# Layer 1's change of sweeps: whose queue stores the finished rows, and which rows are read first

## The chip, the cores and the metric

The kernel runs on one core of a Trainium2 chip. A core has a matrix engine (PE, with its weight loads shown apart as PEld), a vector engine (DVE), an activation engine (ACT), a general engine (POOL) and a sync engine (SP). Each works through its own list of instructions in order and waits on semaphores for the others. Transfers between HBM and the on-chip memory are issued from an engine's queue, here SP's or POOL's, and carried by 16 DMA engines that all queues share. The metric is the device time of one execution in microseconds; lower is better.

## The reference

The program is a two-layer encoder trunk over 2048 rows of 1024 values. Layer 0 is windowed attention beside a gated spatial mixer. Layer 1, which the change touches, is a gated linear recurrence that runs over the sequence in both directions:

```python
def odd_mixer(h, w_in, conv_w, conv_b, w_a, b_a, w_x, b_x, lam, w_out):
    xr, g = jnp.split(h @ w_in, 2, axis=-1)
    xr = centred_depthwise_conv(xr, conv_w, conv_b)
    y = (rg_lru(xr, w_a[0], b_a[0], w_x[0], b_x[0], lam[0], reverse=False)
         + rg_lru(xr, w_a[1], b_a[1], w_x[1], b_x[1], lam[1], reverse=True))
    y = y.astype(h.dtype) * jax.nn.silu(g)
    return y @ w_out
# each layer: x = layer_norm(DEEPNORM_ALPHA * x + gate * mixer(x * (1 + scale) + shift), ln_g, ln_b)
```

`rg_lru` is the scan h[s] = a[s] h[s-1] + b[s]. All of it is in float32; the kernel makes each float32 product from three matmuls of split operands (`mm3`).

## The kernel before

The sequence is cut into four tiles of 512 rows (t = 0 to 3), the width into eight chunks of 128 channels (k or g = 0 to 7). Layer 1 has two sweeps.

**The first sweep** goes forward, t = 0 to 3. For each tile it projects, convolves and computes the gates; it scans forward with the carry from the tile before, and scans backward within the tile, since the carry from behind isn't known yet. For tiles 0 to 2 it stores what the second sweep needs: for even chunks the raw scan inputs (`a_d`, `b_d`), the forward result (`f_d`) and the gate (`g_d`); for odd chunks the finished sum and its carry factor (`u_d`, `v_d`). At the last tile the backward carry is known to be zero, so its rows are finished on the spot by `back(NT - 1, ...)`: DVE multiplies the sum by the gate (line 1034), two columns of it are stored to `y_d` (line 1040, 128 partitions of two values: because of the convolution a tile of scans lies two rows early, so these two belong to tile 2), and ACT and DVE split the other 512 (lines 154 and 155) into the pair `ahi`, `alo` that PE multiplies by the output weights.

**The second sweep** goes backward, t = 2, 1, 0. `load_y(t)` reads a tile back chunk by chunk. An even chunk reads `at`, `bt`, `ft`, `gt` (line 1106), finishes the backward scan on DVE (line 1113), adds on POOL (lines 1116 and 1117), gates on DVE (line 1118); an odd chunk reads `ut`, `vt` and applies the carry on DVE (line 1127). At t = 2 both also read two columns from `y_d` (line 1130). Then ACT and DVE split the result (lines 154, 155). Each name has two buffers, so two chunks of a kind can be ahead. PE then multiplies, for each of four blocks of 128 rows (b) and two halves of the output (n), all eight chunks into one PSUM bank; DVE adds the residual rows `z` (`residual_tile` reads them from `x1_d`, 512 KB each, line 1144; the sums are lines 1164, 1177, 1193) and normalises (`norm_rows`, lines 614 to 625, its last line stores to the output).

**The change of sweeps** lies between them. The program there reads, in this order: the last output weights `wo` are loaded (line 1079), `back(NT - 1, 1, ...)` finishes the second four chunks of tile 3, the memory of the first sweep is given up (`se.close()`) and the pool `op` of the second takes its place, the four residual rows `z` of tile 3 are read, `load_y(2)` follows, and PE's matmuls of tile 3 on chunks 4 to 7.

Loads and stores all go through SP's queue here, in the order of SP's list: an instruction that waits holds what stands behind it. A tile of `op` waits for the last use of whatever lay at its address, and where it lies depends on the order in which names first appear in the pool. The engines' lists are not written by hand: the framework orders each list by its own estimate of when instructions can run, so that a small edit moves instructions on all engines.

Of the kernel before, what the change touches and what calls it, by code (L numbers as in the profile page):

```python
# [20 lines left out]
NT = S // C  # L21
# [32 lines left out]
def kernel(  # L54
# [27 lines left out]
    nc = tc.nc  # L82
# [5 lines left out]
    store = nc.sync.dma_start  # L88
# [24 lines left out]
    y_d = dram.tile([128, KD, 2], F32, name="y_d")  # L113
# [39 lines left out]
    def split(hi, lo, src):  # L153
        act(out=hi, in_=src, func=AF.Copy)  # L154
        tt(out=lo, in0=src, in1=hi.bitcast(F32), op=ALU.subtract)  # L155
# [83 lines left out]
    for i in range(2):  # L239
        nc.gpsimd.dma_start(out=vrow0[24 + 8 * i:32 + 8 * i].rearrange("k (a q) -> k a q", a=4),  # L240
                            in_=ada_b[1, i * D:i * D + D].rearrange("(a k q) -> k a q", a=4, q=32))
# [276 lines left out]
    def act_pair():  # L518
        hi = cp.tile([128, 2, C], F32R, tag="act", bufs=12, name="ahi")
        lo = cp.tile([128, 2, C], F32R, tag="act", bufs=12, name="alo")  # L520
        return hi, lo
# [322 lines left out]
    for t in range(NT):  # L844
        y = sgate(t, hT)
# [41 lines left out]
    def span(t):  # L887
        j0 = 2 if t == 0 else 0
        return j0, (514 if t == NT - 1 else 512) - j0
# [134 lines left out]
    def back(t, s, res, G):  # L1024
        j0, W = span(t)
        w = slice(j0, j0 + W)
        tok = slice(t * C - 2 + j0, t * C - 2 + j0 + W)
        for i in range(4):
            g = 4 * s + i
            if t < NT - 1 and g % 2 == 0:  # L1030
                store(out=g_d[:, g, tok], in_=G[i][:, w])
                continue
            y, A = res[i]
            stt(out=y[:, w], in0=y[:, w], scalar=0.5, in1=G[i][:, w], op0=ALU.mult, op1=ALU.mult)
            if t < NT - 1:
                store(out=u_d[:, g // 2, tok], in_=y[:, w])
                stt(out=A[:, w], in0=A[:, w], scalar=0.5, in1=G[i][:, w], op0=ALU.mult, op1=ALU.mult)
                store(out=v_d[:, g // 2, tok], in_=A[:, w])
                continue
            store(out=y_d[:, g, :], in_=y[:, 0:2])  # L1040
            if i % 2 == 0:
                yp = act_pair()
            split(yp[0][:, i % 2], yp[1][:, i % 2], y[:, 2:514])
            y3[0].append(yp[0][:, i % 2])
            y3[1].append(yp[1][:, i % 2])

    for t in range(NT):
        if t < NT - 1:
            for s in range(2):
                X = x_job(t, hT, s)  # L1050
                if s == 1:
                    nxt = build1(t + 1)
                f = front(t, s, X)
                back(t, s, f, g_job(t, hT, s))
            hT = nxt
        else:
            X0 = x_job(t, hT, 0)
            f0 = front(t, 0, X0)
            X1 = x_job(t, hT, 1)
            f1 = front(t, 1, X1)  # L1060
            sf.close()
            back(t, 0, f0, g_job(t, hT, 0))
            G1 = g_job(t, hT, 1)
# [25 lines left out]
    for k in range(4, KD):  # L1089
        for n in range(2):  # L1090
            resident(oq, n, k)
    back(NT - 1, 1, f1, G1)
    cr = oq.tile([128, NT, KD // 2], F32, name="cr")
    nc.vector.tensor_copy(cr[:, NT - 2], carry_b[:, NT - 1, 1::2])
# [1 line left out]
        tt(out=cr[:, t], in0=first_a[:, t + 1], in1=cr[:, t + 1], op=ALU.mult)  # L1096
        tt(out=cr[:, t], in0=cr[:, t], in1=first_h[:, t + 1], op=ALU.add)

    def load_y(t):
        y = ([], [])  # L1100
        n = C if t < NT - 2 else C - 2
        c0 = t * C

        def fetch(tag, src, k):
            p = op.tile([128, C], F32, tag=tag, bufs=2, name=tag)
            load(out=p[:, 0:n], in_=src[:, k, c0:c0 + n])  # L1106
            return p

        for k in range(KD):
            if k % 2 == 0:  # L1110
                at, bt, ft, gt = (fetch(tag, src, k) for tag, src in (("at", a_d), ("bt", b_d), ("ft", f_d), ("gt", g_d)))
                h = bt[:, 0:n]
                nc.vector.tensor_tensor_scan(out=h[:, ::-1], data0=at[:, 0:n][:, ::-1], data1=h[:, ::-1],  # L1113
                                             initial=carry_b[:, t + 1, k:k + 1], op0=ALU.mult, op1=ALU.add)
                if t > 0:
                    nc.gpsimd.tensor_copy(carry_b[:, t, k:k + 1], bt[:, 0:1])
                nc.gpsimd.tensor_tensor(out=ft[:, 0:n], in0=ft[:, 0:n], in1=h, op=ALU.add)
                stt(out=ft[:, 0:n], in0=ft[:, 0:n], scalar=0.5, in1=gt[:, 0:n], op0=ALU.mult, op1=ALU.mult)
                if t == NT - 2 or k < 4:
                    hi, lo = act_pair()  # L1120
                else:
                    hi, lo = (op.tile([128, 2, C], F32R, tag="act2", bufs=8, name=nm) for nm in ("ahi", "alo"))
            else:
                ft, vt = (fetch(tag, src, k // 2) for tag, src in (("ut", u_d), ("vt", v_d)))
                for u, q0, q1 in ((t, 0, C - 2), (t + 1, C - 2, C)):
                    if u < NT - 1:
                        stt(out=ft[:, q0:q1], in0=vt[:, q0:q1], scalar=cr[:, u, k // 2:k // 2 + 1],  # L1127
                            in1=ft[:, q0:q1], op0=ALU.mult, op1=ALU.add)
            if n < C:
                load(out=ft[:, n:C], in_=y_d[:, k, :])  # L1130
            split(hi[:, k % 2], lo[:, k % 2], ft)
            y[0].append(hi[:, k % 2])
            y[1].append(lo[:, k % 2])
        return y
# [6 lines left out]
    def residual_tile(t, b):  # L1141
        r = t * C + b * 128
        z = op.tile([128, D], F32, tag="z", bufs=6, name="z")
        load(out=z, in_=x1_d[r:r + 128, :])
        return z

    zt = [residual_tile(NT - 1, b) for b in range(4)]
    g_bc = op.tile([128, D], F32, name="g_bc1")
    b_bc = op.tile([128, D], F32, name="b_bc1")
    y2 = load_y(NT - 2)  # L1150
    for k in range(4, KD):
        for n in range(2):
            part_out(ps3[n], wo[n][k], k)
# [14 lines left out]
    zt = [residual_tile(NT - 2, b) for b in range(4)]  # L1168
# [11 lines left out]
    for t in range(NT - 3, -1, -1):  # L1180
        y = load_y(t)
        for b0, n in ((0, 0), (0, 1), (2, 0), (2, 1)):
            for b in (b0, b0 + 1):
                if n == 0:
                    zt[b] = residual_tile(t, b)
                z = zt[b]
                sl = slice(b * 128, b * 128 + 128)
                ps = bank(pj, "pj") if cnt % 8 < 5 else bank(pm, "pm")
                cnt += 1
                cs = slice(n * C, n * C + C)  # L1190
                for k in range(KD):
                    mm3(ps, y[0][k][:, sl], y[1][k][:, sl], wo[n][k][:, 0], wo[n][k][:, 1], k == 0, k == KD - 1)
                stt(out=z[:, cs], in0=z[:, cs], scalar=ALPHA, in1=ps, op0=ALU.mult, op1=ALU.add)
                if n == 1:
                    finish(t, b, z)
# [29 lines left out]
```

## Time and profile before

| | |
|---|---|
| time, median of 3 executions (range) | 1558.17 us (1556.07 to 1564.16) |
| the profiled execution: its time, its span | 1562.55 us, 1560.8 us |
| PE, PEld busy (share of the span) | 95%, 76% |
| DVE, ACT, POOL busy | 76%, 50%, 26% |
| mean granted clock of TensorE | 0.984 |
| DMA, mean rate over the span | 238 GB/s |

The span runs from the first to the last instruction of the profiled execution; the 1.75 us beside it lie outside. An engine's busy share is an average over stages with different limits. What counts is whether PE, which does nearly all the work that can't be moved, stands still, where, and for whom.

### The profile page before, as it was taken

How to read it: one execution, taken by the hardware profiler on the slowest of the kernel's cores; microseconds unless marked ns; L12 is line 12 of the kernel's file. 1: busy time of each engine (PE TensorE's matmuls, PEld its weight loads, DVE VectorE, ACT ScalarE, POOL GpSimd, SP SyncE). 2: the span in 40 equal slices, each digit the busy share in tenths (PEclk: the TensorE clock that was granted, in tenths of full speed). 3: DMA queues.
4: the chain of work that ended last, by engine and by line, in shares of the span. 5: the costliest groups of instructions: out<-in, count | busy, mean ns of one | idle time of the engine just before them, and what ended most of it. 6: DMA issues, size and time to landing. Idle time of an engine off the chain costs nothing. (4 is left out here: it accounts for less than half of the span.)

```text
span 1560.8 us, 22092 instructions
## 1 busy us (share of the span) xinstructions
PE 1481.5 (95%) x7096; PEld 1185.4 (76%) x7096; DVE 1188.0 (76%) x2180; ACT 783.5 (50%) x1470; POOL 405.1 (26%) x488
## 2 busy tenths in 40 slices
PE   7999999989999999999999999999999999987997
PEld 3887777657777777788887777787777788876886
DVE  4599889745769558976776774987987877789996
ACT  4677767542523332343243327499498486851100
POOL 1023233211005000300120232534645523114321
PEclk9999999999999999999999999999999999998999
DMA  9357776849798989988795699788778667439862
GB/s 346 133 170 219 223 198 187 266 131 298 231 293 302 256 252 300 314 268 266 262 298 177 191 246 294 220 267 282 220 239 288 219 214 237 139 146 340 284 202 88
DMA packets 209211, 370.91 MB, mean 238 GB/s; under 512 B 56616, under 2 KB 103620, under 8 KB 209096
## 3 DMA queue, kind: packets, MB, share of 16 engines
q1 hardware_dynamic: 202344, 354.53, 71.1%
q0 software_dynamic: 6752, 14.98, 3.7%
q8 instruction: 56, 0.92, 0.3%
q14 instruction: 59, 0.48, 0.1%
HBM read 261.96 MB, written 85.97 MB: 223 GB/s over the span
## 5 line engine op out<-in xcount | busy, mean ns | idle before, releaser
L154 ACT ACTIVATE hl<-raw 128x512 fp32r<-128x512 f32 x192 | 118.7, 627 | 224.7 <-DMA raw<-in_ev_w_in_dram 139.0
L158 PE MATMUL pj<-ahi,hl 128*128 128x512 f32 x512 | 200.7, 394 | 1.1 <-DVE gz L753 1.1
L159 PE MATMUL pj<-alo,hl 128*128 128x512 f32 x512 | 201.3, 393 | 0.0
L160 PE MATMUL pj<-ahi,hl 128*128 128x512 f32 x512 | 200.8, 394 | 0.0
L155 DVE TENSOR_TENSOR hl<-raw,hl 128x512 fp32r<-128x512 f32 x192 | 131.9, 696 | 74.3 <-ACT hl L154 74.1
L150 POOL TENSOR_SCALAR rstd<-mv 128x1 f32<-128x1 f32 x32 | 27.4, 857 | 401.6 <-DVE mv L616 289.9
L158 PEld LDWEIGHTS pj<-ahi,hl 128*128 128x128 f32 x512 | 97.4, 190 | 22.2 <-DVE gz L753 1.5
L159 PEld LDWEIGHTS pj<-alo,hl 128*128 128x128 f32 x512 | 97.0, 189 | 20.6
L160 PEld LDWEIGHTS pj<-ahi,hl 128*128 128x128 f32 x512 | 97.0, 189 | 20.6
L465 POOL DMA_DIRECT2D P<-T x112 | 62.4, 566 | 178.9 <-DVE nm L430 77.2
L158 PE MATMUL pj<-wqh,hhi 128*128 128x256 f32 (+1 forms) x256 | 88.3, 349 | 2.5 <-ACT hhi L154 1.7
L430 DVE CUSTOM_DVE_ANT_0 P<-psc,mask,nsink 128x384 f32<-128x384 f32 (+1 forms) x128 | 73.9, 595 | 21.7 <-PE psc L429 21.4
L154 ACT ACTIVATE phl<-praw 128x512 fp32r<-128x512 f32 x56 | 35.4, 632 | 108.2 <-DMA praw<-in_od_w_in_dram 56.6
L159 PE MATMUL pj<-wql,hhi 128*128 128x256 f32 (+1 forms) x256 | 87.9, 344 | 0.0
L160 PE MATMUL pj<-wqh,hlo 128*128 128x512 f32 (+1 forms) x256 | 85.3, 345 | 1.4 <-DVE hlo L155 1.4
L977 DVE SCALAR_TENSOR_TENSOR ii<-ii,xc 128x1024 f32<-128x1024 f32 (+2 forms) x32 | 40.6, 1270 | 58.7 <-ACT ii L971 58.7
L433 ACT ACTIVATE P<-P,nm 128x384 f32<-128x384 f32 (+1 forms) x128 | 76.4, 601 | 11.6 <-DVE nm L430 11.4
L777 POOL TENSOR_TENSOR alo<-hm,ahi 128x512 fp32r<-128x512 f32 x32 | 49.7, 1559 | 119.2 <-DVE hm L776 102.7
L947 DVE SCALAR_TENSOR_TENSOR xc<-X,vcol,xc 128x512 f32<-128x512 f32 (+2 forms) x96 | 77.3, 840 | 0.3
L158 PE MATMUL pm<-xhi,hg 128*128 128x512 f32 (+3 forms) x160 | 56.1, 365 | 13.4 <-ACT xhi L154 6.4
L155 DVE TENSOR_TENSOR phl<-praw,phl 128x512 fp32r<-128x512 f32 x56 | 39.1, 699 | 35.4 <-ACT phl L154 32.1
L775 ACT ACTIVATE ahi<-hm,shift,scale 128x512 fp32r<-128x512 f32 x32 | 25.2, 812 | 75.0 <-DVE hm L774 67.1
(304 smaller groups left out, 4319.2 us busy)
## 6 DMA issues: line engine op xcount, KB each, us to landing
hl<-w_d SPq DMA_DIRECT2D x128, 512.0 KB, 4.8
raw<-in_ev_w_in_dram SPq DMA_DIRECT2D x128, 256.0 KB, 3.9
w_d<-phl SPq DMA_DIRECT2D x40, 512.0 KB, 4.7
aw<-in_ada_w_dram SPq DMA_DIRECT2D x32, 512.0 KB, 6.8
hg<-w_d SPq DMA_DIRECT2D x32, 512.0 KB, 4.0
P<-T SPq DMA_DIRECT2D x104, 96.0 KB, 4.7
P<-T POOLq DMA_DIRECT2D x104, 96.0 KB, 4.2
aw<-in_ada_w_dram SPq DMA_DIRECT2D x8, 1024.0 KB, 7.8
```

Source lines behind the costliest of these rows:

```text
L150: nc.gpsimd.tensor_scalar(out=dst, in0=src, scalar1=mul, scalar2=EPS, op0=ALU.mult, op1=ALU.add)
L154: act(out=hi, in_=src, func=AF.Copy)
L155: tt(out=lo, in0=src, in1=hi.bitcast(F32), op=ALU.subtract)
L158: nc.tensor.matmul(ps, lhsT=ahi, rhs=bhi, start=first, stop=False)
L159: nc.tensor.matmul(ps, lhsT=ahi, rhs=blo, start=False, stop=False)
L160: nc.tensor.matmul(ps, lhsT=alo, rhs=bhi, start=False, stop=last)
L430: nc.vector.tensor_tensor_reduce(out=p[:, g, 0:W], in0=ps[:, 0:W], in1=mask[:, m0:m0 + W], scale=-0.125, scalar=nsink[:, h:h + 1], op0=ALU ...
L433: act(out=p[:, g, 0:W], in_=p[:, g, 0:W], func=AF.Exp, scale=-1.0, bias=nm[:, h:h + 1], accum_out=rs[:, h:h + 1])
L465: dma.dma_start(out=pv[32 * r:32 * r + 32, 0:nb, i], in_=T[32 * i:32 * i + 32, 0:nk].rearrange("p (j r) m -> p r j m", r=4)[:, r])
L777: nc.gpsimd.tensor_tensor(out=lo[:, j], in0=h, in1=hi[:, j].bitcast(F32), op=ALU.subtract)
L947: stt(out=xc[:, w], in0=xt[:, j0 + j:j0 + j + W], scalar=vcol1[:, 8 * j + g:8 * j + g + 1], in1=xc[:, w], op0=ALU.mult, op1=ALU.add)
L977: stt(out=ii[i][:, :, w], in0=ii[i][:, :, w], scalar=1.0, in1=xc[:, None, w].to_broadcast([128, 2, W]), op0=ALU.add, op1=ALU.mult)
```

## The change

Line 1040's store is issued from POOL's queue. `load_y` gets a function that it calls after its first pair of chunks; for t = 2 this is what reads the four residual rows of tile 3, which stood ahead of it. `g_bc1` and `b_bc1` get their place after that call.

```diff
-            store(out=y_d[:, g, :], in_=y[:, 0:2])
+            nc.gpsimd.dma_start(out=y_d[:, g, :], in_=y[:, 0:2])
...
-    def load_y(t):
+    def load_y(t, between=None):
...
         for k in range(KD):
+            if k == 2 and between is not None:
+                between()
             if k % 2 == 0:
...
-    zt = [residual_tile(NT - 1, b) for b in range(4)]
+    zt = []
+    y2 = load_y(NT - 2, lambda: zt.extend(residual_tile(NT - 1, b) for b in range(4)))
     g_bc = op.tile([128, D], F32, name="g_bc1")
     b_bc = op.tile([128, D], F32, name="b_bc1")
-    y2 = load_y(NT - 2)
```

The lines behind are numbered two higher (1113 is 1115, 1118 is 1120, 1127 is 1129, 1144 is 1146, 1164 is 1166).

SP's list, from the last weight load to the first loads of the second sweep. Before:

```order
L1079 DMA wo_7_13377<-wo_d_95 128x1024
L1040 DMA y_d<-T 128x2 x2
L1144 DMA z<-x_d 128x1024 x4
L1106 DMA at<-a_d 128x510
L1106 DMA bt<-b_d 128x510
L1106 DMA ft<-f_d 128x510
L1106 DMA gt<-g_d 128x510
```

The same place on SP with the change:

```order
L1079 DMA wo_7_13377<-wo_d_95 128x1024
L1106 DMA at<-a_d 128x510
L1106 DMA bt<-b_d 128x510
L1106 DMA ft<-f_d 128x510
L1106 DMA gt<-g_d 128x510
L1132 DMA ft<-y_d 128x2
L1106 DMA ut<-u_d 128x510
L1106 DMA vt<-v_d 128x510
L1132 DMA ut<-y_d 128x2
L1146 DMA z<-x_d 128x1024 x4
```

The two stores are gone from SP, and the loads of chunks 0 and 1 stand ahead of the four `z`. The stores of all eight chunks are on POOL now; the end of this stage there reads, with the change:

```order
L1017 TENSOR_TENSOR T<-T 128x514 x2
L1040 DMA y_d<-T 128x2 x2
L1017 TENSOR_TENSOR T<-T 128x514 x2
L1040 DMA y_d<-T 128x2 x2
L1118 COPY carry_b<-bt 128x1
L1119 TENSOR_TENSOR ft<-ft,bt 128x510
```

Each pair of stores stands behind the sums (line 1017) that lead to it, and the first of POOL's work for the second sweep stands behind the last pair.

DVE's list, from the last split of tile 3. Before:

```order
L155 TENSOR_TENSOR alo<-T,ahi 128x512
L1164 SCALAR_TENSOR_TENSOR z<-z,pj 128x512 x2
L614 BN_STATS st_13625<-z 128x6
L1164 SCALAR_TENSOR_TENSOR z<-z,pj 128x512
L614 BN_STATS st_13636<-z 128x6
L1113 SCALAR_TENSOR_TENSOR bt<-at,carry_b,bt 128x510
L1164 SCALAR_TENSOR_TENSOR z<-z,pj 128x512 x2
L1164 SCALAR_TENSOR_TENSOR z<-z,pm 128x512 x2
L1127 SCALAR_TENSOR_TENSOR ut<-vt,cr,ut 128x510
```

With the change:

```order
L155 TENSOR_TENSOR alo<-T,ahi 128x512
L1115 SCALAR_TENSOR_TENSOR bt<-at,carry_b,bt 128x510
L1120 SCALAR_TENSOR_TENSOR ft<-ft,gt 128x510
L1129 SCALAR_TENSOR_TENSOR ut<-vt,cr,ut 128x510
L155 TENSOR_TENSOR alo<-ft,ahi 128x512
L155 TENSOR_TENSOR alo<-ut,ahi 128x512
L1166 SCALAR_TENSOR_TENSOR z<-z,pj 128x512
L614 BN_STATS st_13625<-z 128x6
L1166 SCALAR_TENSOR_TENSOR z<-z,pj 128x512 x2
L614 BN_STATS st_13636<-z 128x6
```

Chunks 0 and 1 of tile 2 are finished ahead of all the residual sums of tile 3; they stood between and behind them. From here to the end PE's list differs too: before, 38 matmuls of tile 2 stood ahead of the first that needs chunk 2, and with the change 48, all of chunks 0 and 1 on all eight banks.

## The prediction

> **What bounds the kernel now.** I began with the stretches of engine time around the change of sweeps. Their columns are the stretch, its length, busy time and instructions of PE, PEld, DVE, ACT and POOL, the granted clock, and the DMA share and rate.
>
> ```profile
> 1400.90:1409.90 9.00, 8.95 (x40) 7.07 (x38) 3.30 (x6) 0.00 (x0) 0.00 (x0) 1.00 0.95 350
> 1409.90:1418.00 8.10, 0.00 (x0) 0.00 (x0) 6.80 (x11) 1.26 (x2) 1.44 (x2) 0.64 0.93 296
> 1418.00:1422.40 4.40, 4.37 (x10) 3.51 (x11) 4.40 (x7) 0.63 (x1) 3.08 (x4) 0.50 0.97 308
> 1422.40:1552.60 130.20, 129.62 (x567) 105.92 (x565) 115.65 (x154) 13.29 (x21) 43.38 (x45) 1.00 0.64 222
> 1552.60:1560.80 8.20, 0.00 (x0) 0.00 (x0) 4.42 (x7) 0.00 (x0) 1.69 (x2) 0.68 0.33 128
> ```
>
> PE is full up to 1409.9 us, stands still for 8.1, works for 4.4 at half its clock, and is full again until 1552.6. Only the last normalisation (8.2 us) follows. Whatever the still time loses is therefore lost to the end, provided that PE stays fed afterwards. The timeline of PE and its list of waits name the gap and what ended it:
>
> ```profile
> 1409.46 0.39 PE L160 MATMUL pm<-wo,alo 128*128 128x512 f32 x1
> 1418.03 0.80 PE L158 MATMUL pj<-hl,ahi 128*128 128x512 f32 x1 [8.17 <-ACT ahi L154]
> 1422.44 0.39 PE L158 MATMUL pm<-hl,ahi 128*128 128x512 f32 x1
> 1422.67 0.39 PE L159 MATMUL pm<-hl,ahi 128*128 128x512 f32 x1
> PE pj L160 <- DVE alo L155: 0.6, 2, 0.3
> ```
>
> PE's first matmul of tile 2 waited for ACT's split of chunk 0. Ten matmuls then took from 1418.03 to 1422.44, 0.44 each, and after that one starts every 0.23. So the gap cost 8.17 us and 10 x (0.44 - 0.23) = 2.1 us of slow clock, together 10.3. Next I followed chunk 0 back through the timelines of ACT, DVE, POOL and SP:
>
> ```profile
> 1417.34 0.63 ACT L154 ACTIVATE ahi<-ft 128x512 fp32r<-128x512 f32 x1 [1.16 <-DVE ft L1118]
> 1416.63 0.68 DVE L1118 SCALAR_TENSOR_TENSOR ft<-ft,gt 128x510 f32<-128x510 f32 x1
> 1412.72 1.27 POOL L1117 TENSOR_TENSOR ft<-ft,bt 128x510 f32<-128x510 f32 x1
> 1411.20 1.28 DVE L1113 TENSOR_TENSOR_SCAN bt<-at,carry_b,bt 128x510 f32<-128x510 f32 x1 [1.46 <-DMA bt<-b_d]
> 1402.05 0.32 SPq L1106 DMA_DIRECT2D at<-a_d  x1
> 1402.48 0.60 SPq L1106 DMA_DIRECT2D bt<-b_d  x1
> 1399.94 1.94 SPq L1144 DMA_DIRECT2D z<-x_d  x4
> 1397.58 2.30 SPq L1040 DMA_DIRECT2D y_d<-T  x2
> 1381.99 4.56 SPq L1079 DMA_DIRECT2D wo<-wo_d  x8
> 1398.85 0.69 DVE L1034 SCALAR_TENSOR_TENSOR T<-T,G 128x514 f32<-128x514 f32 x1
> ```
>
> SP had issued the last weights by 1386.55 and then stood until 1397.58 behind the store of two columns, whose rows DVE finished last (line 1034, to 1399.54). Then came 2 MB of `z`, and only at 1402.05 chunk 0, whose `bt` landed at 1411.20, 8.7 after its issue. On DVE the gating of `ft`, ready at 1413.99, stood 2.6 behind residual sums.
>
> **The change, part by part.** *SP freed.* Chunk 0 now stands right behind the weights. The program makes `gt` wait for the first backward scan of tile 3's last pair (line 1007), since `gt` lies where its operand lay:
>
> ```profile
> 1392.40 1.20 DVE L1007 TENSOR_TENSOR_SCAN T<-ra,ii 128x514 f32<-128x514 f32 x1
> gt<-g_d SPq DMA_DIRECT2D x4, 255.0 KB, 6.5
> 1400.24 0.69 DVE L155 TENSOR_TENSOR alo<-T,ahi 128x512 fp32r<-128x512 f32 x1
> 1405.13 0.69 DVE L1164 SCALAR_TENSOR_TENSOR z<-z,pj 128x512 f32<-128x512 f32 x1 [4.20 <-PE pj L160]
> ```
>
> `at`, `bt`, `ft` go at about 1387 and land by 1395.5 even at the 8.7 above. `gt` goes at 1393.6 and lands at 1400.1 by its median of 6.5. DVE is busy with tile 3 until 1400.93 and idled 4.20 us there; it now starts the scan at 1400.93, is through at 1402.2, POOL (0.2 and 1.27) at 1403.7, the gating at 1404.4, ACT at 1405.0. PE is still on tile 3 until 1409.86. Chunk 0 is 4.8 us early: the gap goes, and with it the slow clock. **Removed: 10.3 us.** The eight issues taken from SP (0.32 each) were in its own idle time.
>
> *POOL's stores.* The trace has no such store on POOL. Its nearest rows are POOL's shuffles and larger stores; SP's form lands in 1.4 us:
>
> ```profile
> L465 POOL DMA_DIRECT2D P<-T x112: 536/545/732, 85.1 to 310.7; - x112
> DMA to landing us min/median/max: 2.1/4.1/8.6
> L485 POOL DMA_DIRECT2D o_d<-oq x16: 709/724/843, 106.3 to 340.8; - x16
> 1396.99 1.52 POOL L1017 TENSOR_TENSOR T<-T 128x514 f32<-128x514 f32 x1 [1.31 <-DVE carry_b L1010]
> 1397.47 1.07 DVE L1094 COPY cr<-carry_b 128x4 f32<-128x4 f32 x1
> ```
>
> One store is 0.55 to 0.72 of POOL. Behind the last one (1399.6 to 1400.3) stands POOL's work on chunk 0, which needs DVE's scan at 1402.2: covered. Earlier pairs fall into POOL's waits of 13 us and more. The last two `z` wait on the landing of the last two stores, because they take the memory of those rows: 1402.4 to 1408.9 for the last, 1404.4 by the median of 4.1, which I take since these rows are smaller than either. Behind those `z` stand the loads of chunk 2. No end lies below nothing: a store on POOL saves only SP's issue, in SP's idle time. The rows that earlier stores hold are needed again 20 us later or more.
>
> A rule speaks against it: by the Trainium skill, "SBUF — State Buffer", section "SBUF: two separate sides", a DVE copy in a two-port mode locks POOL out and starves a DMA issued from POOL, 3.1 us for 0.62. The trace agrees on the lock: a DVE copy of 4 columns took 1.07 us while POOL's sum ran. No DVE copy stands beside the last stores, so the sum is unchanged; if it struck, the last `z` would go 2.5 later, from 1404.4 to 1406.9, inside the bounds above.
>
> *What is late next.* PE at 1409.86 has 48 matmuls of chunks 0 and 1, 48 x 0.23 = 10.9 us, and needs chunk 2 at 1420.8. DVE must first do, in its new order, 27 rows from the scan of chunk 0: three scans, two gatings, two carries, two splits, eight residual sums, eight statistics, two small.
>
> ```profile
> L1113 DVE TENSOR_TENSOR_SCAN bt<-at,carry_b,bt 128x510 f32<-128x510 f32 x4 | 5.1, 1272 | 1.5 <-DMA bt<-b_d 1.5
> L614 DVE BATCH_NORM_STATS2 st<-z 128x6 f32<-128x512 f32 x32 | 21.6, 685 | 0.2
> L1164 DVE SCALAR_TENSOR_TENSOR z<-z,pj 128x512 f32<-128x512 f32 x5 | 3.3, 682 | 5.5 <-PE pj L160 5.5
> L1127 DVE SCALAR_TENSOR_TENSOR ut<-vt,cr,ut 128x510 f32<-128x510 f32 x12 | 9.9, 825 | 0.1
> ```
>
> By these means 3 x 1.27 + 20 x 0.68 + 2 x 0.82 + 2 x 0.2 = 19.5; rows overlap by 0.08 (1.28 for a scan, next row 1.20 later), so at least 17.3. With POOL's 1.5 and ACT's 0.63 chunk 2 is ready at 1420.4 to 1422.6: PE waits 0 to 1.8, middle **0.8**. I add no slow clock; the shortest wait with one behind it that I quote is 3.2 (below).
>
> Then DVE as a whole, in two more stretches:
>
> ```profile
> 1400.93:1505.00 104.07, 95.34 (x408) 77.60 (x407) 94.14 (x127) 14.54 (x23) 37.87 (x36) 0.95 0.84 288
> 1461.80:1505.00 43.20, 42.94 (x188) 35.03 (x188) 43.20 (x60) 6.96 (x11) 16.75 (x15) 1.00 0.66 214
> ```
>
> From 1400.93 to 1505 DVE has 94.1 us of work in 104.1, and from 1461.8 on it never rests. If PE is 10.3 earlier, DVE has 93.8 for it, plus POOL's 1.5: it lacks 0.3 + 1.5 = 1.8. PE's new list asks for chunks 2, 4 and 6 of tile 1 later (17, 30 and 61 matmuls later, 4 to 14 us), which covers some. I take **1.5**, between nothing and 4 (1.8, and the 2.3 by which the mean rows exceed the overlapped ones).
>
> The sum: 10.3 - 0.8 - 1.5 = 8.0 us. The profiled execution took 1562.55 us, its span 1560.8; it would take 1554.5. It stands 4.4 above the median of the three runs, and inside their range; as the gap is set by dependences that are the same in every execution, I subtract the same 8.0 from the median 1558.17: **1550.2 us**.
>
> **The rivals.**
>
> *Full gain (1547.9).* DVE catches up in the idle time that its waits for loads leave before 1461.8, and no wait is left: 1558.17 - 10.3. For it: PE's list asks later. Against: DVE's full 43 us.
>
> *Half the gain (1553.4).* A store on POOL lands at the slow end, 8.6 after its issue: the last `z` goes at 1408.9 and lands 6.6 later by its median, at 1415.5. DVE's order holds its sums behind it: from there to the gating of chunk 2 are 13 rows, 8.1 us by the means less their overlap, and ACT, 1424.2, so PE waits 3.4, and with 2.1 of slow clock for such a wait the gain is 10.3 - 5.5 = 4.8. A wait of 3.2 was followed by the slow clock earlier (0.42 us for 256 columns, where 512 take 0.39 at full clock):
>
> ```profile
> z<-x_d SPq DMA_DIRECT2D x16, 512.0 KB, 6.6
> 1370.86 0.39 PE L158 MATMUL pm<-xhi,hg 128*128 128x258 f32 x1 [3.20 <-ACT ra L966]
> 1371.41 0.42 PE L158 MATMUL pm<-xhi,hg 128*128 128x256 f32 x1
> ```
>
> *The gap was smaller in the other runs (1554.6).* The profiled run is 4.4 above the median; if those 4.4 were in this gap, 3.6 remain. Against: PE, ACT and DVE around the gap run at their usual row lengths.
>
> *Slower (1563 to 1578).* SP's list after the change has four output stores (line 625) ahead of loads for tile 1, and a store waits for DVE's last normalisation:
>
> ```profile
> SPq L625 <- DVE z L624: 51.4, 14, 16.0
> ft<-f_d SPq DMA_DIRECT2D x8, 256.0 KB, 5.2
> ```
>
> If one stands its longest 16.0 there, the load behind lands 5.2 later, and POOL, DVE and ACT add 2.5: 23.7 against the 10.9 us of PE's work on a pair of chunks in memory. PE loses 12.8 and 2.1 of slow clock, 14.9: 1558.17 - 10.3 + 14.9 = 1562.8 for one, 1577.7 for two. It decides from a wait of 11.4 on (where 14.9 falls to 10.3). Against: the last of those normalisation rows is the 46th on DVE from the scan of chunk 0, 46 x 0.72 = 33 us at the mean of the 27 rows above (19.5 / 27), so 1434 or a little later, and chunk 0 of tile 1 is needed at 1453.6.
>
> **How the numbers follow.** About 0.5%, 7.8 us, is what a measurement of this kernel can tell from no change. Forecast 0.50; as its 8.0 stands at that bound with terms open to both sides, 0.33 of it is faster and 0.17 the same. Full gain 0.15, faster. Half the gain 0.15, same. Smaller gap 0.08, same. Slower 0.12, of it 0.02 within the bound. So faster 0.48, same 0.42, slower 0.10. The range goes from full gain and the lower run-to-run spread (1547.9 - 2.1 = 1546, rounded) to 1557, which leaves out the slower case and some of the last.
>
> **What would show it.** `at` of chunk 0 issued near 1387 and the `z` after 1396; chunk 0's split on ACT before 1406; no gap on PE at 1409.9 and no stretch at half clock behind; a wait of PE for chunk 2 of 0 to 1.8 near 1421; PE's last matmul near 1544.5. DVE without idle time up to 1500. Wrong would be: a gap over 3 us anywhere after 1409.9 (which of chunk 2's DVE rows or its loads ended it tells the half-gain case from DVE's load), SP's output stores waiting while loads for tile 1 are awaited, or the two last `z` waiting beyond 1405 on POOL's stores.

## The result and the profile after

The changed kernel took 1551.99 us in the median of 20 executions (1544.45 to 1562.19), the kernel before beside it 1559.93 (1553.75 to 1570.07): 7.9 us less, ratio 0.9948 with a 95% interval of 0.993 to 0.9965. That is 0.52%, just at the bound of 0.5% that the prediction put between faster and the same; a ratio of 1 lies outside the interval. 8.0 us were forecast. The profiled execution took 1555.48 us, its span was 1553.6.

First the stretches of engine time, with the columns of the prediction:

```profile
1409.90:1418.00 8.10, 8.10 (x37) 6.74 (x36) 8.10 (x14) 0.00 (x0) 3.16 (x5) 1.00 0.97 321
1418.00:1422.40 4.40, 3.82 (x17) 2.85 (x16) 4.40 (x7) 1.41 (x3) 2.56 (x4) 1.00 1.03 333
1422.40:1545.00 122.60, 120.43 (x528) 98.49 (x526) 111.31 (x147) 12.29 (x20) 45.36 (x41) 1.00 0.64 225
```

PE is busy for all of the 8.1 us in which it stood still before, and the granted clock, 0.64 and 0.50 there before, is 1.00. In the last stretch 2.2 us are missing from PE's time (122.60 less 120.43), where 0.6 were missing before (130.20 less 129.62).

Then the timelines of the changed kernel around the changeover: SP, POOL, DVE, ACT and PE in this order.

```profile
1386.77 0.45 SPq L1106 DMA_DIRECT2D at<-a_d  x1
1394.31 0.32 SPq L1106 DMA_DIRECT2D gt<-g_d  x1
1396.57 8.55 SPq L1146 DMA_DIRECT2D z<-x_d  x4
1405.17 0.43 SPq L1106 DMA_DIRECT2D at<-a_d  x1
...
1400.47 0.54 POOL L1040 DMA_DIRECT2D y_d<-T  x1 [0.82 <-DVE cr L1096]
...
1401.48 1.27 DVE L1115 TENSOR_TENSOR_SCAN bt<-at,carry_b,bt 128x510 f32<-128x510 f32 x1
1404.43 0.69 DVE L1120 SCALAR_TENSOR_TENSOR ft<-ft,gt 128x510 f32<-128x510 f32 x1 [1.67 <-POOL ft L1119]
1407.10 0.68 DVE L1166 SCALAR_TENSOR_TENSOR z<-z,pj 128x512 f32<-128x512 f32 x1
...
1405.16 0.63 ACT L154 ACTIVATE ahi<-ft 128x512 fp32r<-128x512 f32 x1 [4.31 <-DVE ft L1120]
...
1410.10 0.39 PE L160 MATMUL pm<-wo,alo 128*128 128x512 f32 x1
1410.33 0.39 PE L158 MATMUL pj<-hl,ahi 128*128 128x512 f32 x1
1421.95 0.50 PE L158 MATMUL pj<-hl,ahi 128*128 128x512 f32 x1 [0.58 <-ACT ahi L154]
1502.40 0.50 PE L160 MATMUL pj<-wo,alo 128*128 128x512 f32 x1 [0.39 <-DVE alo L155]
1510.18 0.50 PE L158 MATMUL pj<-wo,ahi 128*128 128x512 f32 x1 [1.78 <-ACT ahi L154]
1544.95 0.39 PE L160 MATMUL pm<-wo,alo 128*128 128x512 f32 x1
```

Chunk 0's loads leave at 1386.77 instead of 1402.05, and DVE begins its scan right behind tile 3's last split. ACT has split it by 1405.8, and PE goes from tile 3 (last matmul 1410.10) to tile 2 (1410.33) without a pause. Three waits are left: 0.58 for chunk 2, 0.39 and 1.78 much later.

**One number for the runs below.** Executions of one kernel differ by 10 us and more, and some of that lies ahead of the changeover: tile 3's last matmul started at 1410.10 in this profile of the changed kernel and at 1414.78 in a second one. So beside the ratio each kernel has its *stretch*, the time from the start of tile 3's last matmul to the start of the very last one: here 1544.95 - 1410.10 = 134.85, before 1552.18 - 1409.46 = 142.72. The difference is 7.87. Each stretch is that of one execution; the two profiles of the changed kernel differ by 2.7 us.

### The profile page after: what moved, and what is told of

Its sections match the earlier page's. It is cut to its first block, busy times and chain, and to the rows that moved or that the text cites. A ratio compares the mean times of both kernels' runs of the same rounds, so it can differ in the third digit from the quotient of the medians.

```text
span 1553.6 us, 22105 instructions
## 1 busy us (share of the span) xinstructions
PE 1482.9 (95%) x7096; PEld 1186.6 (76%) x7096; DVE 1187.1 (76%) x2180; ACT 784.1 (50%) x1470; POOL 412.9 (27%) x496
## 5 line engine op out<-in xcount | busy, mean ns | idle before, releaser
L150 POOL TENSOR_SCALAR rstd<-mv 128x1 f32<-128x1 f32 x32 | 32.0, 999 | 410.6 <-DVE mv L616 298.2
```

Source lines behind the costliest of these rows:

```text
L150: nc.gpsimd.tensor_scalar(out=dst, in0=src, scalar1=mul, scalar2=EPS, op0=ALU.mult, op1=ALU.add)
```

## The experiments

The waits are PE's, within the stretch; the slow matmuls are those behind a wait whose successor started over 0.4 us later.

| kernel | ratio to before (95% interval) | stretch, us | PE's waits, us | slow matmuls |
|---|---|---|---|---|
| before | 1 | 142.72 | 8.17, 2 x 0.3 | 10 |
| changed, 1st profile | 0.9948 (0.993 to 0.9965) | 134.85 | 0.58, 0.39, 1.78 | none |
| changed, 2nd profile | 0.994 (0.9927 to 0.9954) | 132.11 | 0.56 | none |
| stores on POOL alone | 0.9983 (0.9965 to 1.0001) | 139.38 | 5.16, 0.3 | 10 |
| reading order alone | 0.9972 (0.9957 to 0.9987) | 137.66 | 2.08, 1.28, 0.6 | 7 |
| changed, stores on ACT | 0.9947 (0.9926 to 0.9967) | 133.57 | 1.12, 0.56 | none |
| changed, sums on DVE | 0.9926 (0.9899 to 0.9954) | 131.46 | none | none |
| the same once more | 0.9938 (0.9917 to 0.9958) | 131.44 | none | none |
| order alone, sums on DVE | 0.9984 (0.9967 to 1.0001) | 137.19 | 1.04, 2.82 | 7 |
| the same, half statistics | 0.9951 (0.9928 to 0.9974) | 132.92 | 1.52 | none |
| changed, statistics twice | 0.9962 (0.9945 to 0.998) | 135.50 | 3.1 in all | none |
| changed, z behind chunk 3 | 0.9951 (0.9932 to 0.9969) | 135.51 | 2.58 | 7 |
| changed, rows stored too | 0.9938 (0.9906 to 0.997) | 133.13 | 1.31 | none |

The two executions without a wait show what PE needs for the stretch: 131.45.

### Each half alone

```diff
 # stores on POOL alone (from the kernel before)
-            store(out=y_d[:, g, :], in_=y[:, 0:2])
+            nc.gpsimd.dma_start(out=y_d[:, g, :], in_=y[:, 0:2])
```

> Only the first half of the change: the two-column stores go by POOL's queue, the four z stay ahead of load_y. In this program the loads at, bt and ft of chunk 0 lie in the memory of finished rows, so at waits until the last two stores of POOL have landed; z lies where nothing is awaited late, and goes right behind the weights near 1387. By the prediction's account (what counts is when chunk 0's loads leave): POOL's last store is issued at 1401.0 in the changed kernel's trace and lands 1.8 (median) to 5.1 later, so at goes near 1402.8, bt lands some 5 us later (no z before it on the queue any more), and scan, POOL's sum, gating and split (1.27 + 1.5 + 0.69 + 0.63) make chunk 0 ready near 1412.5. PE stands about 2.5 instead of 8.2, with 0 to 2.1 of slow clock behind: 3 to 6 us of the 10.3 are gained, ratio to the kernel before 0.996 to 0.998. Rival, the store's queue is the whole effect: as the changed kernel, 0.995. Rival, the order of the loads is the whole effect: at leaves at 1402 as before and lands as late, 1.000.

```diff
 # reading order alone (from the changed kernel)
-            nc.gpsimd.dma_start(out=y_d[:, g, :], in_=y[:, 0:2])
+            store(out=y_d[:, g, :], in_=y[:, 0:2])
```

> Only the second half: the stores stay on SP's queue, the four z are read behind the first pair of tile 2. By the prediction's account: SP still stands until 1397.6 and issues the last two stores by 1399.9; at goes near 1400, bt lands 5.2 later (255 KB without 2 MB ahead; 8.7 with them), at 1405.6; scan 1.27, POOL 1.5, gating 0.69, split 0.63: ready near 1409.7, just when PE is through with tile 3 (1409.9 to 1410.5). So nearly the whole gain stays: PE's gap 0 to 1 us, ratio 0.994 to 0.996, within 1 us of the changed kernel; DVE's order is the same row for row. Rival, SP's standing is what cost the time: PE's gap of 8.2 shrinks only by the 2 us that the z issues took, with the slow clock left, ratio 0.998 to 0.999.

Measured: 0.9983 and 0.9972. Each half brings a part, 1.7 and 2.8 thousandths, and both together 5.2; neither rival, that one half is the whole effect, holds. The ratios alone don't carry this: the first interval reaches 1.0001, and the second (0.9957 to 0.9987) overlaps that of the whole change. PE's waits do (5.16 and 2.08 where it was 8.17, and none at this place with both), in one profile of each half. Both halves brought less than I had expected, the stores by the ratio and by PE's wait (2.5 expected), though their stretch is 3.3 us shorter, within the 3 to 6. The stores on POOL alone, timelines of SP, DVE and PE:

```profile
1386.99 8.22 SPq L1144 DMA_DIRECT2D z<-x_d  x4
1402.39 0.32 SPq L1106 DMA_DIRECT2D at<-a_d  x1
...
1408.95 1.26 DVE L1113 TENSOR_TENSOR_SCAN bt<-at,carry_b,bt 128x510 f32<-128x510 f32 x1
1414.37 0.67 DVE L1118 SCALAR_TENSOR_TENSOR ft<-ft,gt 128x510 f32<-128x510 f32 x1
...
1415.76 0.80 PE L158 MATMUL pj<-hl,ahi 128*128 128x512 f32 x1 [5.16 <-ACT ahi L154]
```

The loads went as expected (at 1402.39 for 1402.8). The scan ended at 1410.2, yet the gating came only at 1414.37: DVE's list puts five residual sums, a carry and a statistics row between them. I had counted 2.2 us from the scan's end to the gating's end; it took 4.8. In this order DVE does its sums when PE's results come, and chunk 0 stands behind.

The reading order alone, SP, DVE and PE:

```profile
1398.04 2.30 SPq L1040 DMA_DIRECT2D y_d<-T  x2
1400.39 0.42 SPq L1106 DMA_DIRECT2D at<-a_d  x1
...
1405.82 1.28 DVE L1115 TENSOR_TENSOR_SCAN bt<-at,carry_b,bt 128x510 f32<-128x510 f32 x1 [4.43 <-DMA ft<-y_d]
1411.56 0.69 DVE L1166 SCALAR_TENSOR_TENSOR z<-z,pj 128x512 f32<-128x512 f32 x1
...
1412.40 0.77 PE L158 MATMUL pj<-hl,ahi 128*128 128x512 f32 x1 [2.08 <-DVE z L1166]
1415.09 0.63 PE L158 MATMUL pj<-hl,ahi 128*128 128x512 f32 x1
1416.56 0.39 PE L160 MATMUL pj<-hl,alo 128*128 128x512 f32 x1
1426.41 0.50 PE L158 MATMUL pj<-hl,ahi 128*128 128x512 f32 x1 [1.28 <-ACT ahi L154]
```

Chunk 0 was split in time, as expected (ACT at 1409.47). But PE waited for something else: DVE's first residual sum (line 1166), which empties the PSUM bank that tile 2's first matmul writes. In this order it stands behind all the rows of chunks 0 and 1, and DVE, which had idled 4.43 us for the loads, was late with them. Behind the wait of 2.08 came slow clock, and chunk 2 came 1.28 late as well. The full change has the same DVE list, row for row there, but starts it 4.3 us earlier (scan at 1401.48, first sum from 1407.10 to 1407.78, 2.5 ahead of PE's 1410.33). **So what the two edits buy together is that DVE begins chunk 0 in the four microseconds in which it idled before.**

### Which queue

```diff
-            nc.gpsimd.dma_start(out=y_d[:, g, :], in_=y[:, 0:2])
+            nc.scalar.dma_start(out=y_d[:, g, :], in_=y[:, 0:2])
```

> The changed kernel with the two-column stores on ACT's queue in place of POOL's. On ACT each stands ahead of the split of the same row, which waits for the same gating, and costs one issue. By the prediction's account any queue that isn't SP's does the same: z goes as early, within 0.5 us of the changed kernel, ratio 0.994 to 0.996. Rival, POOL's own stores cost something (POOL's landing, or a lock beside DVE): 1 to 2 us faster than the changed kernel.

Measured: 0.9947, as the changed kernel's 0.9948; the stretch, 133.57, lies between its two. POOL's queue and ACT's can't be told apart. That `z` goes as early held for the last one only (1404.6 and 1404.8); the first went at 1402.86 instead of 1396.57, which cost PE nothing.

### How late may z be

```diff
-            if k == 2 and between is not None:
+            if k == 4 and between is not None:
```

> The changed kernel with the four z read behind the second pair of tile 2 in place of the first. The z loads go some 4 us later (near 1400.5 to 1405), and DVE's first residual sum, which frees tile 2's first PSUM bank, stands five rows further down (a scan, a gating, a carry, two splits: 3.9 us) than the 1407.1 of the changed kernel: near 1411 to 1412, where PE is through at 1410.3. Theory, DVE's backlog counts and is no larger here (it does chunk 2 while z is on its way): PE waits 1 to 2.5 at tile 2's first matmul, with up to 1.6 of slow clock, and not for chunk 2; stretch from tile 3's last matmul to the last 132.5 to 135.5, ratio 0.994 to 0.9965. Rival, a late z costs as much as in the kernel with the reading order alone (z at 1405.3): 137 to 138, ratio 0.997 to 0.998.

Measured: 0.9951, stretch 135.51. The timelines of SP, DVE and PE:

```profile
1399.84 5.29 SPq L1146 DMA_DIRECT2D z<-x_d  x4
...
1411.72 1.28 DVE L1166 SCALAR_TENSOR_TENSOR z<-z,pj 128x512 f32<-128x512 f32 x2
...
1412.55 0.77 PE L158 MATMUL pj<-hl,ahi 128*128 128x512 f32 x1 [2.58 <-DVE z L1166]
```

As expected: PE waits for the bank (2.58, slightly over the 1 to 2.5) with slow clock behind, and no more for chunk 2. Against the changed kernel's two profiles this costs 0.7 and 3.4 us in the stretch; the ratios don't separate the two.

```diff
-            nc.gpsimd.dma_start(out=y_d[:, g, :], in_=y[:, 0:2])
+            nc.gpsimd.dma_start(out=y_d[:, g, :], in_=y[:, 0:2]); (nc.gpsimd.dma_start(out=row_d[:, i - 2], in_=y[:, 0:512]) if s == 1 and i >= 2 else None)
 # row_d is a new buffer in HBM, 128 x 2 x 512 values
```

> The changed kernel, in which POOL stores the whole rows (512 columns, 256 KB) of the last two groups of tile 3 too, right behind their two columns; the stores go to a place that nobody reads. The last two z take the memory of these rows, and so wait for these stores to land. This makes the half-gain rival of the prediction happen: by POOL's earlier 256 KB stores (4.2 us median to landing) the last z goes near 1406 to 1407, by the slow end (8.6) near 1410. By that rival's account a last z at 1408.9 costs 3.4 of PE's time and 2.1 of slow clock, so 2 to 5.5 us: stretch 134 to 138. Against it: in this program's DVE order the last z is summed as the 17th and 18th row behind chunk 0's scan, near 1413 to 1414, and a z issued at 1406.5 lands (6.6) at 1413: then it costs 0 to 1 us, stretch 132 to 135.

Measured: 0.9938, stretch 133.13, no wait for the bank or for chunk 2. The timeline of SP:

```profile
1409.88 0.99 SPq L1146 DMA_DIRECT2D z<-x_d  x2
```

This execution was 4.3 us later as a whole (tile 3's last matmul at 1414.40). The last z went 3.9 us ahead of that matmul, in the changed kernel 5.3 ahead. So 1.4 us of the margin were used up without a loss, but the half-gain rival's case (1.0 ahead) wasn't reached; its price stays untested.

### What sets the later waits

The prediction put them down to DVE's volume of work. Two tests of it:

```diff
-        for n in range(2):
+        for n in (0, 1, 0, 1) if twice else (0, 1):
             nc.vector.bn_stats(st6[:, n, :], z[:, n * C:n * C + C])
 # twice for tiles 3 and 2
```

> The changed kernel with the statistics (line 614) of the rows of tiles 3 and 2 computed twice: 16 more DVE rows of about 0.6, some 10 us more work for DVE between 1400.9 and 1505, where it is busy for 99.3 of 104.1. By the prediction's account (DVE as a whole sets PE's later waits): the idle 4.8 are used up and PE waits 5 to 8 us more than in the changed kernel (2.75), 0.999 to 1.001 of the kernel before. Rival, the later waits come from single chains and their order, and DVE has room: at most 2 us more, ratio 0.995 to 0.9965.

Measured: 0.9962, stretch 135.50: 0.7 and 3.4 us more than the changed kernel's two stretches, not 5 to 8. That is nearer to the rival. But the test is weaker than it was meant to be. In 150 us around the stretch the statistics rose from 21.3 to 31.3 us, yet DVE's busy time only from 136.4 to 142.0: other rows became shorter at the same time (line 1129 in all from 16.2 to 13.1).

```diff
-                nc.gpsimd.tensor_tensor(out=ft[:, 0:n], in0=ft[:, 0:n], in1=h, op=ALU.add)
+                tt(out=ft[:, 0:n], in0=ft[:, 0:n], in1=h, op=ALU.add)
```

> The changed kernel with the sum of the forward and the backward part (line 1119, 12 times for tiles 2 to 0) on DVE in place of POOL. In the changed kernel's trace ten DVE rows beside POOL's sums are longer than their kind, together by 7.9 us, and POOL's sums take 1.28 to 3.01. Theory A, DVE and POOL hold each other up there: twelve sums of about 0.6 to 0.68 cost DVE 7.2 to 8.2 and give back the 7.9, so DVE is no fuller, and the chain scan, sum, gating gets shorter by 0.6 to 2.3 each time: PE's three later waits (0.58, 0.39, 1.78) shrink to under 1 us together, 1 to 2.5 us faster than the changed kernel, ratio 0.993 to 0.994. Rival B, the long rows are long for another reason and DVE is simply 7.2 to 8.2 fuller: from 1400.9 to 1505 it has 4.8 us of idle time, so PE waits 2.5 to 5 us more, ratio 0.997 to 0.998.

> The changed kernel with the twelve sums on DVE, once more beside the changed kernel itself. Theory (a sum on POOL lengthens the DVE row beside it by as much as the sum costs on DVE): no PE wait after 1410, no DVE row longer than its kind, and 1.5 to 3.5 us less than the changed kernel. Rival, the first comparison was spread between executions: within 1 us of the changed kernel.

Measured: 0.9926 and 0.9938, and PE waited nowhere in the stretch, in both profiles. First, in the changed kernel, two of POOL's sums with the DVE rows beside them:

```profile
1435.86 2.27 POOL L1119 TENSOR_TENSOR ft<-ft,bt 128x510 f32<-128x510 f32 x1
1436.97 1.71 DVE L1129 SCALAR_TENSOR_TENSOR ut<-vt,cr,ut 128x510 f32<-128x510 f32 x1
1438.68 2.35 POOL L1119 TENSOR_TENSOR ft<-ft,bt 128x512 f32<-128x512 f32 x1
1439.80 1.77 DVE L1120 SCALAR_TENSOR_TENSOR ft<-ft,gt 128x510 f32<-128x510 f32 x1
```

Rows of 0.68 take 1.7, and POOL's sum of 1.28 takes 2.3. The longest sum of POOL, and the last of the DVE rows that ran one behind the other at its start:

```profile
1421.24 3.01 POOL L1119 TENSOR_TENSOR ft<-ft,bt 128x510 f32<-128x510 f32 x1
1422.42 0.68 DVE L155 TENSOR_TENSOR alo<-ft,ahi 128x512 fp32r<-128x512 f32 x1
```

The sum ended at 1424.25, 1.28 after 1422.97: it seems to have begun only when DVE was through with that row (1423.10). Now the groups of DVE rows of line 1129 from the start of chunk 0 on, of the changed kernel:

```profile
L1129 DVE SCALAR_TENSOR_TENSOR ut<-vt,cr,ut 128x510 f32<-128x510 f32 x12 | 12.4, 1029 | 1.5 <-DMA ut<-u_d 1.5
L1129 DVE SCALAR_TENSOR_TENSOR ut<-vt,cr,ut 128x2 f32<-128x2 f32 x8 | 3.8, 473 | 0.0
```

and with the sums on DVE:

```profile
L1129 DVE SCALAR_TENSOR_TENSOR ut<-vt,cr,ut 128x510 f32<-128x510 f32 x12 | 8.8, 731 | 0.7 <-DMA ut<-u_d 0.7
L1129 DVE SCALAR_TENSOR_TENSOR ut<-vt,cr,ut 128x2 f32<-128x2 f32 x8 | 1.7, 211 | 0.0
L1119 DVE TENSOR_TENSOR ft<-ft,bt 128x512 f32<-128x512 f32 x8 | 5.4, 674 | 0.0
L1119 DVE TENSOR_TENSOR ft<-ft,bt 128x510 f32<-128x510 f32 x4 | 2.7, 686 | 0.1
```

Twelve sums of 8.1 us came to DVE. Line 1129 alone gave back 12.4 + 3.8 - 8.8 - 1.7 = 5.7, and the stretches show that DVE as a whole is no fuller (the changed kernel, then the one with the sums on DVE):

```profile
1400.90:1505.00 104.10, 103.13 (x450) 84.45 (x451) 99.31 (x137) 13.97 (x23) 40.33 (x41) 1.00 0.81 281
```

```profile
1400.00:1503.60 103.60, 103.58 (x454) 85.21 (x455) 99.57 (x151) 14.52 (x23) 22.89 (x28) 1.00 0.81 283
```

DVE is busy for 99.3 and for 99.6 us, and PE waits in the one and not in the other. The changed kernel's second profile says the same: over the 104.1 us that match (1405.58 to 1509.68) DVE was busy for 100.8, and PE had no late wait. So the volume isn't the cause. What changed is the chain from scan to gating: there DVE's list stood for POOL's sum, 2.9 us in all in either profile of the changed kernel, and nothing here. By the Trainium skill, "SBUF — State Buffer", section "SBUF: two separate sides", DVE and GpSimd share a pair of ports as an exclusive lock, which a DVE instruction with two SBUF inputs takes against a GpSimd one that reads SBUF. The traces agree: the rows of lines 1129, 1120 and 155 have two SBUF operands, and either they or the sum stood until the other was through. A residual sum of line 1179, which reads `z` from SBUF and `pm` from PSUM, lay beside POOL's sum at 1454.12, and both kept their usual lengths (0.68 and 1.29).

Is this version faster than the changed kernel? In the stretch by 0.65 and 3.4 us. By the medians of executions it isn't settled:

> The changed kernel itself once more, beside the runs below: ratio to the kernel before 0.993 to 0.9965 as measured, its PE waits after 1410 near 2.7 us in all (0.58, 0.39, 1.78 in the first trace).

Measured: 0.994 for the changed kernel, beside 0.9938 with the sums on DVE; the first time it was 0.9948 and 0.9926. The changed kernel's second profile had no wait at 1502 or 1510. So the 2.2 us of late waits in its first profile don't come in every execution. Where the two part can be seen on DVE, whose rows stand in the same order. In the first:

```profile
1487.97 2.00 DVE L1129 SCALAR_TENSOR_TENSOR ut<-vt,cr,ut 128x510 f32<-128x510 f32 x2 [1.47 <-DMA ut<-u_d]
```

This `ut` landed 6.2 us after its issue, and DVE stood 1.47 for it; in the second it landed after 4.9, and DVE didn't wait. Then the second row of this pair, two columns that take 0.21, took 1.33 beside POOL's sum, and not in the second. Counted from tile 3's last matmul, DVE in the first was already 1.3 us behind the second ahead of this load, and 3.7 behind at the gating for which PE waited at 1510 (1508.80; 1509.78 in the second). The late load and the row held up beside POOL's sum account for 2.4 of these 3.7; where the 1.3 came from stays open. In the two profiles with the sums on DVE, DVE stood 0.7 and 0.9 us for loads at the same line, and PE waited nowhere.

### The order alone, again

```diff
 # reading order alone, and:
-                nc.gpsimd.tensor_tensor(out=ft[:, 0:n], in0=ft[:, 0:n], in1=h, op=ALU.add)
+                tt(out=ft[:, 0:n], in0=ft[:, 0:n], in1=h, op=ALU.add)
```

> The reading order alone (stores left on SP's queue), with the twelve sums on DVE. In the trace of the reading order alone PE waited 2.08 us for the PSUM bank that DVE's first residual sum frees, had eight matmuls at half clock behind it (0.43 each instead of 0.23: 1.6 us), and waited 1.28 us for chunk 2. The first residual sum stood behind chunk 0's rows on DVE, among them 1.65 us of waiting for POOL's sum. If the DVE order behind chunk 0 is the cause, a sum of 0.6 on DVE brings this 1.05 us forward: the wait falls to about 1.0, without slow clock (a wait of 1.78 had none in the changed kernel), the wait for chunk 2 to 0.3: 3 to 4 us less than the reading order alone, ratio 0.993 to 0.995. Rival, the late z loads are the cause: the wait stays near 2, with its slow clock, ratio 0.996 to 0.997.

Measured: 0.9984, stretch 137.19. The miss is instructive:

```profile
1405.07 1.28 DVE L1115 TENSOR_TENSOR_SCAN bt<-at,carry_b,bt 128x510 f32<-128x510 f32 x1 [4.42 <-DMA ft<-y_d]
1423.24 0.66 DVE L1120 SCALAR_TENSOR_TENSOR ft<-ft,gt 128x510 f32<-128x510 f32 x1
...
1410.66 0.47 PE L158 MATMUL pj<-hl,ahi 128*128 128x512 f32 x1 [1.04 <-DVE z L1166]
1424.62 0.50 PE L158 MATMUL pj<-hl,ahi 128*128 128x512 f32 x1 [2.82 <-ACT ahi L154]
```

The bank's wait fell from 2.08 to 1.04, just as worked out. But PE, which started earlier, came earlier to chunk 2, and DVE had not a pause from 1405.07 to chunk 2's gating at 1423.24: the wait went there, and the slow clock with it. Is it DVE's backlog or chunk 2's loads?

```diff
-        for n in range(2):
+        for n in range(1 if half else 2):
             nc.vector.bn_stats(st6[:, n, :], z[:, n * C:n * C + C])
 # half for tile 3 alone; the aggregate then reads one half
```

> The reading order alone with the sums on DVE (the kernel that waited 1.04 us for the bank and 2.82 for chunk 2), with the statistics of tile 3's rows taken over the first 512 columns only: the rows of tile 3 are normalised with half their statistics, and four DVE rows of 0.6 are gone ahead of chunk 2's gating. From tile 3's last matmul to the last matmul that kernel took 137.2 us, where the changed kernel took 134.9 and 132.1 and the one with the sums on DVE 131.4. Theory, DVE's backlog (it began chunk 0 at 1405.1 instead of 1401.5, after 4.4 us of idle time, and had no pause until chunk 2's gating at 1423.2): four rows fewer, and a scan that now stands behind, bring that gating 2.4 to 3.6 us forward, the wait of 2.82 and its 1.6 of slow clock go, the stretch falls to 132.5 to 133.5, ratio 0.9945 to 0.996. Rival, chunk 2's loads (issued 1406.7 to 1413.2) are late: the wait stays over 2, 136 to 137, ratio 0.997 to 0.9985.

Measured: 0.9951, stretch 132.92, no wait for chunk 2:

```profile
1413.78 0.47 PE L158 MATMUL pj<-hl,ahi 128*128 128x512 f32 x1 [1.52 <-DVE z L1166]
1414.09 0.40 PE L159 MATMUL pj<-hl,ahi 128*128 128x512 f32 x1
```

It is the backlog: from chunk 0's scan to chunk 2's gating DVE took 14.6 us (1408.19 to 1422.80) where it had taken 18.2, with four statistics rows less and a scan that now stands behind, and the wait is gone, although the loads go as late. In these runs DVE's work counted where it stood ahead of a row that PE was about to need, and not by its sum over 100 us.

## Why the prediction was right, step by step

**The gap, 10.3 us: right.** Chunk 0's `at` at 1386.77 (1387 forecast), `gt` at 1394.31 (1393.6), the split at 1405.16 (before 1406), PE without a pause and without slow clock. The changed kernel's first profile ran some 0.6 us later than the one before at this place; the steps agree within that.

**POOL's stores: right.** A store took 0.55 in the median (0.55 to 0.72 forecast). Its landing was 1.8 us in the median of all eight, where I took 4.1. But the two on which the last `z` wait are the slow ones: they landed after 5.1 and 3.9 (4.3 and 3.1 in the second profile), SP stood 6.7 us for them, and the last `z` went when I had it (1404.8, against 1404.4). In the kernel with the stores on POOL alone, the same two landed after 1.7. There the DMA engines' share was 0.01 from 1399 to 1401, here 0.91; that the loads ahead of them made them slow is likely and wasn't tested.

```profile
L1040 POOL DMA_DIRECT2D y_d<-T x8: 537/548/683, 1327.0 to 1400.5; - x8
DMA to landing us min/median/max: 1.7/1.8/5.1
```

**Chunk 2's wait, 0.8: right.** It was 0.58 and 0.56, without slow clock. From chunk 0's scan to the end of chunk 2's gating DVE took 19.8 us (1401.48 to 1421.24), where the 27 rows and POOL's sum had been put at 18.8 to 21.0.

**DVE as a whole, 1.5: the size came near by luck, the reason didn't hold.** The later waits were 2.2 us in one profile and nothing in the other. That DVE lacks time up to 1505, as the step had it, is refuted: it was busy for 99.3 of 104.1 us in the profile with the waits and for 100.8 in the one without, and the sign "without idle time up to 1500" didn't come. In place of it the two profiles show single chains: a load that landed late, and a row and POOL's sum that held each other up. That POOL's sum is needed for the waits is likely, as there was none in two profiles without it; it isn't proved, as the changed kernel's second profile lacked the late ones too. So it is luck in part that the total came out at 7.9 for 8.0; the second comparison gave 10.1.

**A step that was missing.** The prediction asked only when chunk 0 and chunk 2 are ready. PE's first matmul of tile 2 needs a free bank too, and so DVE's first residual sum, through at 1407.8 in the changed kernel, 2.5 us ahead of PE. It didn't decide here; in the reading order alone and with z later it was the first wait (2.08 and 2.58). My expectation for the reading order alone failed on it.

**The rivals.** Full gain (1547.9) came nearest in the second comparison: 1553.77 against 1563.84, 10.1 us. The slower rival didn't come: SP's output stores went from 1431.55 on, and PE waited for nothing in tile 1. The half-gain case was not reached in any run. Whether the gap was smaller in the other executions of the kernel before, no trace shows, as it was profiled once; gains of 7.9 and 10.1 us by the medians speak against the 3.6 of that rival.

## What to carry to other kernels

Where two edits each cut the same lateness, ask which engine idles, and with what it could be filled: here DVE had four free microseconds, and only chunk 0's rows could fill them, and either edit alone gave a third to a half of what both gave. When a wait goes, list everything that the next matmul needs, the PSUM bank as much as the operands. And before calling an engine full, look whether its rows are longer than their kind: a sum on POOL that "costs nothing" may cost the neighbour as much as doing it there.

## What was not expected of the hardware

**Slow clock after short waits.** In the stretch, waits of PE of 0.56 to 1.78 us (1.12, 1.28, 1.52 and 1.78 among them) had full clock behind them; those of 2.08, 2.58 and 2.82 had a stretch of matmuls at 0.43 us instead of 0.23, some 1.6 us more in all, and those of 5.16 and 8.17 had ten. The Trainium skill, "TensorE: Matmul & The Clock Gate", "Part 1: The HAM clock gate (the "warmup" mystery)", names an idle window of about 3.4 us; in these traces two thirds of it were at times enough, and the slow stretch itself lasted 3.4 to 4.4 us.

These waits give no threshold, though. Each of the thirteen executions has one more wait of 2.10 to 2.16 us, for ACT's `xhi` (line 154) between 1230 and 1240. The mean granted clock of the 3.2 us behind it was 1.00 in three of them (the changed kernel both times, and `z` behind chunk 3) and 0.50 to 0.74 in the other ten. And a wait of 2.77 at 468.23 in the kernel before had full clock behind it. So whether slow clock follows a wait of 2.1 to 2.8 us can differ between executions, and the 1.6 us that it cost three of the runs above need not be there in the next.

**What a POOL sum costs DVE.** Ten DVE rows beside POOL's sums in the changed kernel's first profile were together 9.2 us longer than their kind, 0.7 to 1.1 each (7.9 in the expectation was too low); with the sums on DVE no row was.
